# Strassen sums S3 and S4 kept in PSUM, a second copy of the high parts there, and a reordered entrance to the gate GEMM, in one decoder layer

## The chip, the cores and the metric

One core of a Trainium2 chip runs the whole program. The metric is the device time of one execution in microseconds (us); the kernel before has a median of 2184.21 us over 3 runs (2181.18 to 2185.54).

## The reference

One step of a hybrid layer with width D = 2048, for 512 prompt tokens and 8 x 4 sample tokens, 544 in all. Only the second half matters here:

```python
mixed = concat(rms_norm(a, g_attn), rms_norm(s, g_ssm)) @ w_out      # 2048 x 2048
x = x + mixed
hf = rms_norm(x, g_ffn)
x = x + (silu(hf @ w_gate) * (hf @ w_up)) @ w_down                   # D_FF = 5632
y = rms_norm(x, g_final)
```

## The kernel before

**Tokens and halves.** All 544 tokens stand in the columns of a tile of 128 x 544 (a `slot`), as two halves of 272 (`L_` and `R_`), so that one half fills part of one PSUM bank. A matrix product is made of fp32r matmuls of a 128 x 128 weight block with 272 columns.

**Two parts of each number.** Every operand is split in two: a high part (`Copy` into an fp32r tile on ScalarE) and a low part (the number less its high part, a `tensor_tensor` on VectorE). A product is high x high + high x low + low x high, three matmuls.

**Strassen units.** The products with `w_gate`, `w_up` and `w_down` use Strassen's scheme with seven products (`P1` to `P7`) over 2 x 2 blocks. The left sides of four of them are sums of weight blocks: S1 (`P5`) and S2 (`P6`) are made on GpSimd (`PT`), S4 (`P7`) and S3 (`P3`) on VectorE (`TT`), all in `sadd`; `P1`, `P2` and `P4` take raw blocks. A unit is one product over a half of the inner dimension: in the gate and up GEMMs 12 matmuls, 8 with the high part of its weights and then 4 with the low part. A `Gem` of gate or up has the 14 units of `TWO`, one of down the 7 of `ONE`. Two `Gem`s, gate and up, make a pair, and there are 22 pairs, 616 units.

**Order.** Nothing is scheduled at run time: each engine runs its instructions in the order in which the program writes them, and semaphores hold an instruction until its inputs and its buffer are ready. `stage` writes unit after unit: first what `at` holds for the unit (work on the results of earlier `Gem`s, and the splits of their sums), then the sums of a unit some places ahead (`sadd`, by `AHEAD`), the unit's matmuls (`mms`), the results that it completes (`events`: copies on ScalarE, `tensor_tensor` on VectorE), the conversion of the unit two places ahead (`conv(u + 2)`: high part, then low part), and a hook.

**Buffers.** High and low parts have three buffers each (`whi`, `wlo`), so `conv(u + 2)` needs the matmuls of unit u - 1 to be done. Sums lie in the four buffers of the tag `raw` (`sa`), but that of `P6` for the second half, which has a `slot`. Raw weights (`rw`, three buffers of 1 MB in two transfers of 512 KB) are fetched by SyncE; `conv` of a `P4` unit issues the next fetch, into the buffer whose last reader is a low part of `P4`. From the `w_out` product on, PSUM's eight banks are shared out as six for products (`mm`) and two for the rest (`ps`). A `Gem` holds three banks, X, Y and V; a pass over two column blocks of `w_out` (`gemm_pair`) takes four, and its results leave them by `tensor_tensor` on VectorE (`evac_wa`, `evac_ws`).

**The entrance.** `w_out` is done in eight passes over the attention half and eight over the state-space half, 96 matmuls each. After each of the latter, two row blocks of x get their sums and their Strassen forms (`make_forms`), and their squares go to `accA`. During the last pass unit 0 of the gate is converted, units 1 and 2 after it. `rstd_bcast` at unit 10 sums `accA` over partitions on TensorE and makes 1/sqrt of the mean (`rbf`, the tile `rbc`): two `tensor_scalar`, `Sqrt` on ScalarE, one reciprocal of 128 x 544 and four more VectorE instructions for a Newton step.

## Time and profile before

| what | us |
|---|---|
| median of 3 runs (lowest, highest) | 2184.21 (2181.18, 2185.54) |
| the profiled execution, its own time | 2186.86 |
| its span from first to last instruction | 2185.0 |
| first matmul of the gate, first of down | 686.0, 1669.6 |
| the `w_out` passes | 480 to 686 |
| TensorE, VectorE, GpSimd, ScalarE busy in the span | 2062.3, 1865.6, 1156.2, 1087.9 |

The span is the profile's; the execution's own time has 1.86 us more around it. "Busy" of TensorE is that of pipelined matmuls, so that a busy TensorE can still be one that started late. A row of a group has the source line, the engine, the operation, the tile written and the tiles read by their names in the program (`wh` high part, `wl` low part, `rw` raw weights, `sa` a sum, `s` a slot, `mm` and `ps` PSUM banks).

### The profile page before, as it was taken

How to read it: one execution, taken by the hardware profiler on the slowest of the kernel's cores; microseconds unless marked ns; L12 is line 12 of the kernel's file. 1: busy time of each engine (PE TensorE's matmuls, PEld its weight loads, DVE VectorE, ACT ScalarE, POOL GpSimd, SP SyncE). 2: the span in 40 equal slices, each digit the busy share in tenths (PEclk: the TensorE clock that was granted, in tenths of full speed). 3: DMA queues.
4: the chain of work that ended last, by engine and by line, in shares of the span. 5: the costliest groups of instructions: out<-in, count | busy, mean ns of one | idle time of the engine just before them, and what ended most of it. 6: DMA issues, size and time to landing. Idle time of an engine off the chain costs nothing.

```text
span 2185.0 us, 43831 instructions
## 1 busy us (share of the span) xinstructions
PE 2062.3 (94%) x16370; PEld 2003.8 (92%) x16370; DVE 1865.6 (85%) x2825; ACT 1087.9 (50%) x2277; POOL 1156.2 (53%) x1012
## 2 busy tenths in 40 slices
PE   8497999999998999999999999999999999999996
PEld 7497899879988899999999999999999999999996
DVE  7988845668577899999999999999988888888987
ACT  6132336765254455455555555455554545544564
POOL 7715442123275566666666666666655555555600
PEclk9798999999998999999999999999999999999998
DMA  6354793214343244434443454435349988977554
GB/s 178 98 149 148 220 294 113 76 55 130 110 135 117 78 159 142 143 123 140 161 145 120 129 173 133 133 129 173 126 145 322 329 288 280 346 267 240 191 162 144
DMA packets 331646, 368.46 MB, mean 169 GB/s; under 512 B 55473, under 2 KB 260249, under 8 KB 331417
## 3 DMA queue, kind: packets, MB, share of 16 engines
q1 hardware_dynamic: 330536, 363.92, 51.3%
q8 instruction: 129, 2.11, 0.4%
q0 software_dynamic: 640, 1.48, 0.2%
q14 instruction: 85, 0.69, 0.1%
q10 hardware_dynamic: 256, 0.26, 0.0%
HBM read 277.67 MB, written 88.52 MB: 168 GB/s over the span
## 4 chain that ended last, share of the span: by engine, by line
PE 69%; DVE 12%; issue 4%; ACT 2%; POOL 1%; DMA 1%; DVEq 0%; SPq 0%; ACTq 0%; POOLq 0%
PE mm L2009 52%; PE mm L293 14%; DVE wl L1995 4%; DVE s L388 1%; DVE sa L1976 1%; DVE sa L1978 1%; DVE wl L263 1%; POOL s L2283 1%; PE ps L1368 0%; PE ps L1626 0%; PE ps L1620 0%; ACT wh L261 0%; DMA rw<-in_w_gate_dram 0%; POOL accA L342 0%; DMA s<-fd 0%
## 5 line engine op out<-in xcount | busy, mean ns | idle before, releaser
L2009 PE MATMUL mm<-s,wh 128*128 128x272 f32 x7056 | 1040.2, 289 | 9.8 <-ACT wh L1994 4.5
L2009 PEld LDWEIGHTS mm<-s,wh 128*128 128x128 f32 x7056 | 946.5, 189 | 17.0 <-ACT wh L1994 8.8
L2009 PE MATMUL mm<-s,wl 128*128 128x272 f32 x3528 | 597.6, 291 | 20.3 <-DVE wl L1995 19.8
L293 PE MATMUL mm<-s,wh 128*128 128x272 f32 x2816 | 503.3, 298 | 36.8 <-DVE u L1158 13.5
L2009 PEld LDWEIGHTS mm<-s,wl 128*128 128x128 f32 x3528 | 499.6, 189 | 35.0 <-DVE wl L1995 34.9
L1995 DVE TENSOR_TENSOR wl<-sa,wh 128x512 fp32r<-128x512 f32 (+1 forms) x468 | 473.3, 1016 | 42.2 <-ACT wh L1994 36.8
L1995 DVE TENSOR_TENSOR wl<-rw,wh 128x512 fp32r<-128x512 f32 (+1 forms) x384 | 409.8, 1076 | 66.3 <-ACT wh L1994 62.5
L293 PEld LDWEIGHTS mm<-s,wh 128*128 128x128 f32 x2816 | 415.0, 194 | 48.2 <-issue 18.3
L1994 ACT ACTIVATE wh<-sa 128x512 fp32r<-128x512 f32 (+1 forms) x468 | 291.0, 623 | 262.6 <-PE mm L2009 108.3
L293 PE MATMUL mm<-s,wl 128*128 128x272 f32 x1408 | 314.6, 294 | 16.9 <-DVE wl L263 16.8
L1994 ACT ACTIVATE wh<-rw 128x512 fp32r<-128x512 f32 (+1 forms) x384 | 238.5, 621 | 143.2 <-PE mm L2009 96.7
L1972 POOL TENSOR_TENSOR sa<-rw 128x512 f32<-128x512 f32 (+1 forms) x128 | 204.6, 1599 | 163.9 <-DMA rw<-in_w_gate_dram 52.0
L293 PEld LDWEIGHTS mm<-s,wl 128*128 128x128 f32 x1408 | 232.8, 193 | 19.9 <-DVE wl L263 19.8
L261 ACT ACTIVATE wh<-raw 128x512 fp32r<-128x512 f32 x200 | 124.2, 625 | 164.7 <-PE mm L293 104.3
L263 DVE TENSOR_TENSOR wl<-raw,wh 128x512 fp32r<-128x512 f32 x152 | 122.8, 813 | 73.0 <-ACT wh L261 72.8
L388 DVE TENSOR_TENSOR s<-s,s 128x544 fp32r<-128x544 f32 (+2 forms) x154 | 142.7, 943 | 33.6 <-ACT s L387 27.1
L2082 POOL TENSOR_TENSOR s<-s,rbc 128x544 f32<-128x544 f32 x66 | 114.9, 1754 | 72.6 <-ACT s L2085 72.6
L1974 POOL TENSOR_TENSOR sa<-sa,rw 128x512 f32<-128x512 f32 (+1 forms) x84 | 138.9, 1653 | 3.2
L342 POOL TENSOR_TENSOR wl<-raw,wh 128x512 fp32r<-128x512 f32 x48 | 64.5, 1346 | 138.6 <-ACT wh L261 128.2
L342 POOL TENSOR_TENSOR s<-s,s 128x512 f32<-128x512 f32 (+3 forms) x67 | 79.0, 1190 | 58.2 <-ACT s L921 36.5
L2180 POOL TENSOR_TENSOR s<-s,s 128x272 f32<-128x272 f32 x40 | 30.9, 773 | 130.4 <-ACT s L2179 130.4
L1976 DVE TENSOR_TENSOR sa<-rw 128x512 f32<-128x512 f32 (+1 forms) x128 | 96.9, 757 | 0.0
(350 smaller groups left out, 2112.4 us busy)
## 6 DMA issues: line engine op xcount, KB each, us to landing
rw<-in_w_gate_dram SPq DMA_DIRECT2D x88, 512.0 KB
rw<-in_w_up_dram SPq DMA_DIRECT2D x88, 512.0 KB
rw<-in_w_down_dram SPq DMA_DIRECT2D x72, 512.0 KB
fd<-s SPq DMA_DIRECT2D x133, 272.0 KB
s<-fd SPq DMA_DIRECT2D x133, 272.0 KB
x2d<-s SPq DMA_DIRECT2D x80, 272.0 KB
s<-x2d SPq DMA_DIRECT2D x80, 272.0 KB
raw<-in_w_in_dram SPq DMA_DIRECT2D x72, 256.0 KB
```

Of the source, the lines that this page charges most:

```text
L261: nc.scalar.activation(out=hi[:, :nk], in_=t[:, :nk], func=AF.Copy)
L263: eng.tensor_tensor(out=lo[:, :nk], in0=t[:, :nk], in1=hi[:, :nk].bitcast(F32), op=ALU.subtract)
L293: nc.tensor.matmul(ps[mt][h][:, :HALF], lhsT=w, rhs=x[:, h * HALF:(h + 1) * HALF], start=st, stop=sp)
L342: return f(*a, **kw)
L388: nc.vector.tensor_tensor(out=lo, in0=src, in1=hi.bitcast(F32), op=ALU.subtract)
L1972: PT(out=v, in0=blk(g, h, 1, 0), in1=blk(g, h, 1, 1), op=ALU.add)
L1974: PT(out=v, in0=g.S[h], in1=blk(g, h, 0, 0), op=ALU.subtract)
L1976: TT(out=v, in0=blk(g, h, 0, 0), in1=blk(g, h, 1, 0), op=ALU.subtract)
L1994: nc.scalar.activation(out=hv, in_=src, func=AF.Copy)
L1995: TT(out=lv, in0=src, in1=hv.bitcast(F32), op=ALU.subtract)
L2009: nc.tensor.matmul(ps[:, :HALF], lhsT=w[:, j, :], rhs=x, start=new and i == 0, stop=last and i == len(todo) - 1, skip_group_check=True)
L2082: return lambda: PT(out=gt[t], in0=gt[t], in1=rbf, op=ALU.mult)
```

## The change

The sums for `P7` and `P3` go to a bank of `ps` in place of a `raw` buffer. In gate and up, ScalarE writes the high part of a raw block (`P1`, `P2`, `P4`) a second time, to a `ps` bank, and VectorE's subtraction reads it there. The pools become five `mm` and three `ps` banks. At the entrance, units 0 and 1 are converted during the last `w_out` pass; the last row blocks get a form routine of their own (`last`), which puts half of the forms and the squares behind the first units; `rstd_bcast` is written out in six hooks at units 8 to 13, with the reciprocal in two halves and its two partition sums in `mm` banks; and one multiplication by `rbf` in the first gate is planned three units later.

```diff
--- before.py
+++ after.py
@@ -1964,7 +1964,9 @@
     def sadd(u):
         g, p, h, _, _ = units[u]
         n = g.halves[h][1]
-        if (p, h) == ("P6", 1):
+        if p in ("P7", "P3"):
+            v = bank()[:, :n * P].rearrange("p (a c) -> p a c", c=P)
+        elif (p, h) == ("P6", 1):
             v = slot()[:, :n * P].rearrange("p (a c) -> p a c", c=P)
         else:
             v = v128(stream.tile([P, NK, 256], F32, tag="raw", name=nm("sa"), bufs=4), n)
@@ -1992,7 +1994,12 @@
         lo = stream.tile([P, NK, 256], F32R, tag="wlo", name=nm("wl"))
         hv, lv = v128(hi, n), v128(lo, n)
         nc.scalar.activation(out=hv, in_=src, func=AF.Copy)
-        TT(out=lv, in0=src, in1=hv.bitcast(F32), op=ALU.subtract)
+        if p in ("P1", "P2", "P4") and len(g.halves) == 2:
+            hp = bank()[:, :n * P].rearrange("p (a c) -> p a c", c=P)
+            nc.scalar.activation(out=hp, in_=hv.bitcast(F32), func=AF.Copy)
+        else:
+            hp = hv.bitcast(F32)
+        TT(out=lv, in0=src, in1=hp, op=ALU.subtract)
         conv_t[u] = hv, lv
         if p == "P4":
             raw_dma()
@@ -2088,7 +2095,7 @@
             TT(out=ut[1][:, L_], in0=g.b["X"][:, :HALF], in1=gt[1][:, L_], op=ALU.mult)
 
         def post_gate(u0):
-            plan_at(u0 + 11, lambda: PT(out=gt[1][:, R_], in0=gt[1][:, R_], in1=rbf[:, R_], op=ALU.mult))
+            plan_at(u0 + (14 if f == 0 else 11), lambda: PT(out=gt[1][:, R_], in0=gt[1][:, R_], in1=rbf[:, R_], op=ALU.mult))
             plan_at(u0 + 15, silu(1), None, scale(1), None, scale(0), None, silu(0), None, scale(0))
 
         def post_up(u0):
@@ -2294,6 +2301,27 @@
                     steps[:] = make_forms(xg[0], xg[1], e, xforms[m0 // 2])
                     steps[0]()
                 steps = []
+                if m0 == 14:
+                    def last():
+                        b0, b1 = xg
+                        t, v = slot(), slot()
+                        a, bh, bl, th, tl, vh, vl = (slot(F32R) for _ in range(7))
+                        split((a[:, L_], a[:, R_]), b0[:, L_])
+                        TT(out=t[:, L_], in0=b0[:, R_], in1=b0[:, L_], op=ALU.subtract)
+                        split((th[:, L_], tl[:, L_]), t[:, L_])
+                        TT(out=t[:, R_], in0=b1[:, R_], in1=t[:, L_], op=ALU.subtract)
+                        split((th[:, R_], tl[:, R_]), t[:, R_])
+                        xforms[7].extend([a, bh, bl, th, tl, vh, vl])
+
+                        def rest0():
+                            TT(out=v[:, L_], in0=b1[:, R_], in1=b0[:, R_], op=ALU.subtract)
+                            TT(out=v[:, R_], in0=b1[:, L_], in1=t[:, R_], op=ALU.subtract)
+                            split((vh, vl), v)
+                        at.setdefault(1, []).append(rest0)
+                        at.setdefault(2, []).append(lambda: split((bh, bl), b1))
+                        at.setdefault(3, []).append(squares)
+                    deferred.append(last)
+                    return
                 deferred.append(forms)
                 deferred.append(lambda: steps[1]())
                 deferred.append(lambda: steps[2]())
@@ -2302,8 +2330,8 @@
 
     es_ps.close()
     es_ps2 = ExitStack()
-    pools["mm"] = es_ps2.enter_context(tc.tile_pool(name="mm2", bufs=6, space=PSUM))
-    pools["ps"] = es_ps2.enter_context(tc.tile_pool(name="ps2", bufs=2, space=PSUM))
+    pools["mm"] = es_ps2.enter_context(tc.tile_pool(name="mm2", bufs=5, space=PSUM))
+    pools["ps"] = es_ps2.enter_context(tc.tile_pool(name="ps2", bufs=3, space=PSUM))
     AXP = Pairs(ah, al)
     for m in range(0, 16, 2):
         for mt in range(2):
@@ -2336,12 +2364,11 @@
             if k == 2:
                 for u in sum_at.pop(-1):
                     sadd(u)
-            if k == 6:
-                conv(0)
+            if k in (4, 6):
+                conv(k // 2 - 2)
 
         run(gemm_pair(SXP, evac_ws(m), pre_piece=first_units if m == 14 else None))
-    for u in range(1, 3):
-        conv(u)
+    conv(2)
     flush()
     probe("x2", x2[0])
 
@@ -2352,7 +2379,36 @@
     nc.sync.dma_start(out=v_s[0, :, 0:124].rearrange("b r h d -> b (r h d)"),
                     in_=cache_v[0, :, 4:128].rearrange("b r h d -> b (r h d)"))
 
-    units[0][0].hooks[10] = lambda: rstd_bcast(rbf, accA, D)
+    rs = {}
+
+    def rs_sum():
+        rs["p"] = [bank("mm"), bank("mm")]
+        for x in range(2):
+            nc.tensor.matmul(rs["p"][x][:, :HALF], lhsT=ones, rhs=accA[:, x * HALF:(x + 1) * HALF], start=True, stop=True)
+
+    def rs_mean():
+        rs["m"], rs["t"] = slot(), slot()
+        for x in range(2):
+            TSC(out=rs["m"][:, x * HALF:(x + 1) * HALF], in0=rs["p"][x][:, :HALF], scalar1=1.0 / D, scalar2=EPS,
+                op0=ALU.mult, op1=ALU.add)
+        nc.scalar.activation(out=rs["t"], in_=rs["m"], func=AF.Sqrt)
+
+    def rs_rec(x):
+        return lambda: nc.vector.reciprocal(out=rbf[:, x * HALF:(x + 1) * HALF], in_=rs["t"][:, x * HALF:(x + 1) * HALF])
+
+    def rs_newton(i):
+        def go():
+            m, t = rs["m"], rs["t"]
+            if i == 0:
+                TT(out=t, in0=rbf, in1=rbf, op=ALU.mult)
+                TT(out=t, in0=t, in1=m, op=ALU.mult)
+            else:
+                TSC(out=t, in0=t, scalar1=-0.5, scalar2=1.5, op0=ALU.mult, op1=ALU.add)
+                TT(out=rbf, in0=rbf, in1=t, op=ALU.mult)
+        return go
+
+    for i, f_ in enumerate((rs_sum, rs_mean, rs_rec(0), rs_rec(1), rs_newton(0), rs_newton(1))):
+        units[0][0].hooks[8 + i] = f_
     stage(0, nU - 3)
     WS.limit = len(pieces)
     w_dma(nextp[0] + 1)
```

In rows of the program's order the numbers behind a name tell one tile from another. The first place is VectorE in a gate `Gem`, from the low part of `P6`'s first half to that of `P2`'s second half. Before:

```order
L1995 TENSOR_TENSOR wl_9313<-sa_9205,wh_9312 128x512
L1978 TENSOR_TENSOR sa_9317<-rw_8935,sa_9205 128x512
L1995 TENSOR_TENSOR wl_9334<-s_9277,wh_9333 128x512
L1976 TENSOR_TENSOR sa_9340<-rw_8935 128x512
L1995 TENSOR_TENSOR wl_9356<-sa_9317,wh_9355 128x512
L1976 TENSOR_TENSOR sa_9360<-rw_9159 128x512
L1995 TENSOR_TENSOR wl_9375<-sa_9340,wh_9374 128x512
L388 TENSOR_TENSOR s_9379<-s_9177,s_9379 128x272
L1995 TENSOR_TENSOR wl_9397<-sa_9360,wh_9396 128x512
L1995 TENSOR_TENSOR wl_9414<-rw_9159,wh_9413 128x512
```

With the change:

```order
L2002 TENSOR_TENSOR wl_9346<-sa_9232,wh_9345 128x512
L1980 TENSOR_TENSOR ps_9350<-rw_8944,sa_9232 128x512
L2002 TENSOR_TENSOR wl_9367<-s_9310,wh_9366 128x512
L1978 TENSOR_TENSOR ps_9373<-rw_8944 128x512
L2002 TENSOR_TENSOR wl_9389<-ps_9350,wh_9388 128x512
L1978 TENSOR_TENSOR ps_9393<-rw_9184 128x512
L2002 TENSOR_TENSOR wl_9408<-ps_9373,wh_9407 128x512
L388 TENSOR_TENSOR s_9412<-s_9202,s_9412 128x272
L2002 TENSOR_TENSOR wl_9430<-ps_9393,wh_9429 128x512
L2002 TENSOR_TENSOR wl_9447<-rw_9184,ps_9449 128x512
```

Order and count are the same. The sums of `P3` and `P7` are now written to `ps`, the low parts of `P3` and `P7` read that bank, and the low part of `P2` reads the second copy of the high part in place of the high part; those of `P6` read two SBUF tiles as before.

The second place is ScalarE at the end of an up `Gem` and the start of the next gate: the high parts of `P3`, `P4`, `P1`, `P5`, `P2` and `P1`. Before:

```order
L1994 ACTIVATE wh_9180<-sa_9141 128x512
L1994 ACTIVATE wh_9198<-rw_8878 128x512
L1994 ACTIVATE wh_9219<-rw_8935 128x512
L1994 ACTIVATE wh_9236<-sa_9162 128x512
L1994 ACTIVATE wh_9256<-rw_8935 128x512
L1994 ACTIVATE wh_9273<-rw_9159 128x512
```

With the change, from the same high part on:

```order
L1996 ACTIVATE wh_9205<-ps_9164 128x512
L1996 ACTIVATE wh_9223<-rw_8894 128x512
L1999 ACTIVATE ps_9226<-wh_9223 128x512
L1996 ACTIVATE wh_9246<-rw_8944 128x512
L1999 ACTIVATE ps_9249<-wh_9246 128x512
L1996 ACTIVATE wh_9265<-sa_9187 128x512
L1996 ACTIVATE wh_9285<-rw_8944 128x512
L1999 ACTIVATE ps_9288<-wh_9285 128x512
```

Behind the high part of each raw block stands its second copy (L1999); what came behind it stands one place later.

The third place is VectorE at the first 1/sqrt, around units 11 to 15 of the first gate. Before:

```order
L1995 TENSOR_TENSOR wl_8875<-rw_8198,wh_8874 128x512
L1995 TENSOR_TENSOR wl_8900<-sa_8860,wh_8899 128x512
L1770 TENSOR_SCALAR s_8905<-ps_8903 128x272
L1770 TENSOR_SCALAR s_8905<-ps_8904 128x272
L400 RECIPROCAL rbc<-s_8906 128x544
L401 TENSOR_TENSOR s_8906<-rbc 128x544
L402 TENSOR_TENSOR s_8906<-s_8906,s_8905 128x544
L403 TENSOR_SCALAR s_8906<-s_8906 128x544
L404 TENSOR_TENSOR rbc<-rbc,s_8906 128x544
L2062 TENSOR_TENSOR s_8896<-mm_8736,s_8783 128x272
L1995 TENSOR_TENSOR wl_8932<-rw_8337,wh_8931 128x512
```

With the change:

```order
L2002 TENSOR_TENSOR wl_8889<-rw_8198,ps_8891 128x512
L2392 TENSOR_SCALAR s_8897<-mm_8870 128x272
L2392 TENSOR_SCALAR s_8897<-mm_8871 128x272
L2002 TENSOR_TENSOR wl_8921<-ps_8874,wh_8920 128x512
L2397 RECIPROCAL rbc<-s_8898 128x272
L2069 TENSOR_TENSOR s_8917<-mm_8736,s_8791 128x272
L2002 TENSOR_TENSOR wl_8939<-rw_8337,ps_8941 128x512
L2397 RECIPROCAL rbc<-s_8898 128x272
L2002 TENSOR_TENSOR wl_8963<-rw_8503,ps_8965 128x512
L2403 TENSOR_TENSOR s_8898<-rbc 128x544
L2404 TENSOR_TENSOR s_8898<-s_8898,s_8897 128x544
L2072 TENSOR_TENSOR s_8917<-mm_8713,s_8846 128x272
```

The reciprocal is two instructions of 272 columns, and between the parts of the computation stand results (L2069, L2072) and low parts of the units that follow.

## Rows read from the trace of the kernel before

**Rows 1.** Gate and up: busy us and count of PE, PEld, DVE, ACT, POOL.

```profile
730.60:1669.60 939.00, 925.93 (x7202) 907.54 (x7201) 877.57 (x981) 488.37 (x896) 603.61 (x419) 1.00 0.44 145
```

**Rows 2.** Strassen matmuls and weight loads by stretch; granted clock behind the counts.

```profile
686.00:730.60 44.60, 32.02 (x192) 30.70 (x193) 0.81 0.24 83
730.60:1669.60 939.00, 925.93 (x7202) 907.54 (x7201) 1.00 0.44 145
1700.00:2000.00 300.00, 300.00 (x2399) 300.00 (x2398) 1.00 0.87 299
...
1021.48:1029.08 7.60, 7.05 (x50) 6.21 (x49) 1.00 0.00 1
```

**Rows 3.** Waits, 860 to 1640 us: total us, times, longest.

```profile
PEld mm L2009 <- DVE wl L1995: 23.0, 56, 1.4
...
PE mm L2009 <- DVE wl L1995: 10.5, 29, 1.2
PEld mm L2009 <- ACT s L2054: 3.4, 16, 0.5
```

**Rows 4.** Timeline, up to a gate's units 4 to 8: start, duration, instruction.

```profile
1006.36 1.78 DVE L1995 TENSOR_TENSOR wl<-rw,wh 128x512 fp32r<-128x512 f32 x1
...
1010.00 0.94 SPq L1951 DMA_DIRECT2D rw<-in_w_gate_dram  x2
...
1015.45 1.29 POOL L1972 TENSOR_TENSOR sa<-rw 128x512 f32<-128x512 f32 x1 [3.18 <-DVE wl L1995]
...
1023.88 1.09 POOL L2117 TENSOR_TENSOR s<-s,s 128x272 f32<-128x272 f32 x1
...
1024.40 0.77 PE L2009 MATMUL mm<-s,wl 128*128 128x272 f32 x4 [0.26 <-DVE wl L1995]
...
1026.64 1.77 DVE L1995 TENSOR_TENSOR wl<-sa,wh 128x512 fp32r<-128x512 f32 x1
```

**Rows 5.** By line, 860 to 1640 us: count, shortest, median, longest in ns.

```profile
L2062 DVE TENSOR_TENSOR s<-mm,s x35: 426/428/430, 877.4 to 1623.9; 128x272 f32<-128x272 f32 x35
...
L1995 DVE TENSOR_TENSOR wl<-sa,wh x251: 676/1032/1853, 859.4 to 1639.2; 128x512 fp32r<-128x512 f32 x126
L1995 DVE TENSOR_TENSOR wl<-rw,wh x212: 676/948/1789, 860.4 to 1629.4; 128x512 fp32r<-128x512 f32 x106
...
L1994 ACT ACTIVATE wh<-rw x212: 613/632/637, 861.1 to 1639.3; 128x512 fp32r<-128x512 f32 x106
```

**Rows 6.** Timeline of the entrance and of the first 1/sqrt.

```profile
692.88 2.18 PE L2009 MATMUL mm<-s,wh 128*128 128x272 f32 x8 [3.44 <-ACT wh L1994]
...
698.49 1.39 PE L2009 MATMUL mm<-s,wh 128*128 128x272 f32 x8
...
717.01 3.55 DVE L400 RECIPROCAL rbc<-s 128x544 f32<-128x544 f32 x1 [0.72 <-ACT s L399]
...
718.65 1.16 PE L2009 MATMUL mm<-s,wh 128*128 128x272 f32 x8
...
724.82 1.27 PE L2009 MATMUL mm<-s,wl 128*128 128x272 f32 x4 [5.01 <-DVE wl L1995]
```

**Rows 7.** Timeline of results leaving the banks at two ends of `w_out` passes.

```profile
506.30 0.67 PE L293 MATMUL mm<-s,wh 128*128 128x272 f32 x4
...
508.58 0.78 DVE L1859 TENSOR_TENSOR s<-mm,s 128x272 f32<-128x272 f32 x2
...
509.07 0.99 PE L293 MATMUL mm<-s,wh 128*128 128x272 f32 x4 [1.11 <-DVE s L1859]
...
629.27 0.67 PE L293 MATMUL mm<-s,wh 128*128 128x272 f32 x4
...
630.86 1.47 DVE L2280 TENSOR_TENSOR s<-mm,rbc 128x272 f32<-128x272 f32 x4
```

**Rows 8.** Timeline of a last-chunk down `Gem`.

```profile
2014.01 2.17 DVE L1995 TENSOR_TENSOR wl<-sa,wh 128x384 fp32r<-128x384 f32 x2
...
2017.97 0.99 PE L2009 MATMUL mm<-s,wh 128*128 128x272 f32 x6 [0.41 <-DVE s L2192]
```

## The prediction

> **What bounds the kernel now.** I read first how long the Strassen matmuls take in each stretch, then who was waited for, then the timeline where the waits lie.
>
> In down, from 1700 to 2000 us, TensorE is busy for all of 300 us over 2399 matmuls, 125 ns each [rows 2]; 12 of them, a unit that waits for nothing, take 1.50 us (I use 1.504, with which units in a row follow each other). The 600 units of gate and up from 730.6 us on would take 902.4 us and take 939.0 [rows 2]: 36.6 us are lost, 1.71 a pair. The first 16 units, from 686.0 to 730.6, take 44.6 us in place of 24.1: 20.5 lost, at a granted clock of 0.81, so a part of them ran at the lower of its two levels, 1.2 and 2.4 GHz [rows 2].
>
> The waits name one thing: between 860 and 1640 us TensorE and its weight loads waited for a low part made on VectorE (10.5 and 23.0 us; the two overlap), and 3.4 us for a result leaving bank X [rows 3]. VectorE is busy for 877.6 of 939.0 us [rows 1], 20.5 us in a `Gem` whose matmuls need 21.1.
>
> The loss sits in one place. The four gate units from 1021.48 to 1029.08 (`P6`, `P6`, `P3`, `P7`) take 7.60 us, 1.58 over their four times 1.504 [rows 2], nearly a pair's whole loss. There VectorE's instructions and GpSimd's sums alternate, and VectorE's instructions of 512 columns last up to 1.8 us [rows 4].
>
> **Reading from PSUM.** Low parts of 512 columns last 676 ns at the shortest, with a median of 948 to 1032 and up to 1853; results with one operand in PSUM (272 columns) last 426 to 430 ns in all 35 cases, although GpSimd is busy 64% of this time [rows 1, 5]. So an instruction with two SBUF operands is held up by GpSimd, one with a PSUM operand is not. A 512-column low part that reads PSUM isn't in the trace: it costs 0.68 us if it is never held, 1.03 if nothing changes; I take 0.68, since the PSUM rows have no spread at all. Per `Gem`, six low parts of raw blocks go from 0.95 to 0.68 and those of `P7` and `P3`, four, from 1.03: 3.0 us of VectorE's 20.5.
>
> The Trainium skill (SBUF — State Buffer, Who interferes with whom) has it that a VectorE instruction with two SBUF inputs and a GpSimd instruction that reads SBUF exclude each other for a whole instruction, while one with at most one SBUF input stays out of it. By that rule, which the trace bears out, the low parts of `P5` and `P6` and the sums themselves stay as long as they are; that is the second case below.
>
> **Gate and up: -30.** Only what ends last counts. (a) `P7`'s low part at 1026.64 took 1.77 us, against a sum of GpSimd, and TensorE got it 0.55 late [rows 4]. At 0.68 it is in time: 0.55 of the 1.58, safe. (b) The other 1.0 hangs on `P6`'s second low part, still two SBUF operands, which TensorE got 0.4 late at 1024.40, and on what queues behind it: `P3`'s low part, and ScalarE's copy of X, which stands behind a high part that waits for a sum. It was slow because GpSimd's chain of sums ran until 1024.97 (L2117). That chain starts when the gate's second raw block has landed, 1015.45 (L1972; the profile names a low part that ended at that moment, but other sums of this line wait for the fetch by name), and its fetch was issued at 1010.00, behind `P4`'s low part of the up `Gem` [rows 4]. In front of that low part stand a low part of 1.78 us [rows 4] and others of the same kind, now 0.68 each, less 0.6 for the second copy: the fetch goes out some 1.5 us sooner, the chain ends near 1023, and the low part then needs no alternating. It would be ready at about 1023.6, needed at 1024.0. That leaves little room, so I leave 0.3 of a pair's 1.7: 1.4 x 21.4 pairs = 30 us. Bounds: (a) alone, 0.55 x 21.4 = 12; everything, 36.6.
>
> **What the second copies cost: 0.** Six copies of 0.63 us [rows 5] a `Gem` take ScalarE from 488 of 939 us [rows 1] to some 650, 72% of the shorter stage. A raw unit's chain is high part 0.63, copy 0.63, low part 0.68; it starts when a `whi` buffer comes free, two units before its own, and its low part is wanted 8 matmuls into that unit: 2 x 1.50 + 1.0 = 4.0 us for 1.9 of work. That slack of 2 us is the cover. How long an ACTIVATE into PSUM or a VectorE sum into PSUM lasts the trace doesn't show: 0.40 times 512/272 = 0.75 would be the nearest guess from the 272-column copies, and even a copy twice as long stays inside the slack. A bank of `ps` comes round after three allocations, ten a `Gem`, so each is free two units after its use; if VectorE is that late, ScalarE stands, and the copies of X, Y behind it too.
>
> **Entrance: -5.5.** Unit 1 began at 692.88, after 3.44 us without work, because its high part stood behind the last pass's results [rows 6]. Now units 0 and 1 run before that gap and unit 2 starts there, 1.5 us won. But the forms behind it now go to and fro between VectorE and ScalarE piece by piece (sum, high part, low part), so unit 3 starts late: unit 2's high part, copy and low part end at 694.1, four sums and two splits of 272 columns follow at 0.43 each with 0.4 of ScalarE between, and the high part is ready at about 698.8, where unit 3 started at 698.49 [rows 6]. That takes the gain back. The squares' two ScalarE instructions and half of the forms stand behind units 3 and 4, worth 1 to 2: I take 1.5 (0 to 6). At the 1/sqrt the reciprocal of 3.55 us and what follows it kept a low part back for 5.01 us [rows 6], after which the clock was low; units 13 to 15 took from 718.65 [rows 6] to 730.6, 7.4 more than their 4.5. The same work, 8 us, is now spread over five units, of which each leaves VectorE about 0.9 us beside a lead of 2; by that some 3.5 us of stalls remain, each near 1 us, as long as those in gate and up [rows 3], where the clock stays at 1.00 [rows 2]. So -4 (-2 to -7). The two partition sums take `mm` banks, but bank X of the next `Gem` gets a bank that is free by then.
>
> **`w_out` with five banks: +3.3.** A pass needs four banks at once. With six, a pass's first two were always free; with five, its second matmul waits for the first result of the pass before. That result left at 509.01 (508.58 plus 0.43) where the pass began at 506.30: a wait of 2.6, in place of one 13 matmuls on that ended at 509.07 [rows 7]. At 630.86 plus 0.43 it is 1.9 for a pass begun at 629.27, where 1.0 was lost anyway. Going so through the 15 boundaries, seven wait more than before: 1.0, 0.3, 0.25, 0.7, 0.9, 0 (a wait that comes later takes it in) and 0.2, together 3.3. Bounds: 0, if the waits behind take them in, and 16 times the longest.
>
> The Trainium skill (Perfetto Trace Analysis, Optimizing Tensor Performance, on matmuls) wants groups that don't depend on each other to rotate through different banks, so that one's results leave during the next one's matmuls, and five banks for passes of four go against it. By the rule each boundary is exposed, the third case; the rows above show seven of them that are.
>
> **Down: -3.** In the last chunk's eight `Gem`s, TensorE waits 0.41 us for a result queued on VectorE behind low parts (2.17 us for two, at 2014.01) [rows 8]. These two are `P7` and `P3`, now PSUM: 8 x 0.4 = 3.2. Bounds 0 and 3.3.
>
> **Sum.** -30 - 5.5 + 3.3 - 3 = -35. From the profiled execution (2185.0 span, 1.86 around it, 2186.9) that is 2151.7; the median of the runs is 2.65 lower: **2149**.
>
> **The rivals.**
> 1. As summed, 2149: 0.60.
> 2. VectorE stays the bound in the gate's four units, because low parts of `P5` and `P6`, form splits and sums still alternate with GpSimd: (a) alone, -12.4, entrance -5.5, `w_out` +3.3, down 0: -14.6, 2170. For it: the five VectorE instructions that end with the first late low part all keep two SBUF operands. Against: GpSimd's chain starts sooner. 0.22.
> 3. Slower: the banks. If each of the 16 `w_out` passes waits as long as the worst (2.6 us), 42 us are lost in place of 3.3: 2188. It ends on that side from an average of 2.4 us a pass. Against: most results left within 0.5 us of their last matmul. 0.05.
> 4. The change doesn't do what it says, since PSUM operands of 512 columns or copies into PSUM are slow, and low parts come as late as before: entrance and `w_out` only, -2: 2182. 0.07.
> 5. All of it: -36.6 - 12 + 3.3 - 3 = -48, 2136. 0.06.
>
> Cases 1, 2 and 5 are faster by over 0.2% (4.4 us, about what can be told from no change here): 0.88; within, 0.07; slower, 0.05. The range goes from the last case with a few us of spread, 2132, to the second, 2173; case 1 alone has 2138 to 2160.
>
> **What would show it.** Right: low parts from `rw` and `ps` at 0.68 without spread, those of `P5`, `P6` still spread; the waits for low parts in gate and up down from 23 to under 6 us; the stage from the first matmul of the gate to the first of down down from 983.6 to about 948; unit 2 starting where unit 1 did; no wait of 5 us at the reciprocal; new short waits for VectorE's results at `w_out` boundaries. Wrong: copies into PSUM well over 0.7 us, ScalarE waiting for `ps` banks, or GpSimd's chain still ending after the low part of `P6`.

## The result

The changed kernel takes 2145.97 us (median of 4 runs, 2141.46 to 2146.99) against 2183.94 of the kernel before beside it: a ratio of 0.9823, 95% interval 0.9806 to 0.9841. The prediction was 2149 in a range of 2132 to 2173.

The profiled execution has a span of 2143.9 us. These are windows of its Strassen matmuls, cut at the first matmul of gate unit 0, unit 16, unit 28 (the second pair) and of down, then one window of the `w_out` matmuls. Behind the length of each stand busy time and count of PE and PEld, the granted clock, the DMA share and GB/s:

```profile
684.64:722.22 37.58, 29.09 (x192) 27.27 (x193) 0.91 0.21 71
722.22:742.81 20.59, 18.84 (x147) 18.19 (x146) 1.00 0.21 62
742.81:1632.66 889.85, 888.73 (x7058) 886.32 (x7057) 1.00 0.45 151
1632.66:2038.12 405.46, 402.97 (x3194) 402.09 (x3192) 1.00 0.83 283
```

```profile
474.45:684.64 210.19, 200.75 (x1536) 198.46 (x1536) 0.97 0.41 129
```

The 21 pairs from unit 28 on are 588 units, 884.4 us without a loss. Before, they took 939.0 [rows 2] less 18.0 for units 16 to 27, that is 921.0, or 1.74 lost a pair; now it is 889.9, or 0.26. Set beside the terms of the prediction:

| stretch | before | after | difference | predicted |
|---|---|---|---|---|
| `w_out` | 207.05 | 210.19 | +3.1 | +3.3 |
| gate units 0 to 27 (the entrance) | 62.65 | 58.17 | -4.5 | -5.5 |
| 21 pairs | 921.0 | 889.85 | -31.1 | -30 |
| down | 408.8 | 405.46 | -3.3 | -3 |

These come to -35.8, where -35 was forecast. The profiled spans differ by 5 us more, 4.5 of it ahead of `w_out`, which the change doesn't touch: that stretch took 479.0 us in the profile of before, 474.5 here, 472 to 479 in the experiments.

The waits over 780 us of gate and up, as long as [rows 3] (total us, times, longest):

```profile
POOL sa L1974 <- DVE wl L2002: 7.7, 3, 3.2
...
PEld mm L2016 <- DVE wl L2002: 1.4, 2, 0.7
PE mm L2016 <- DVE wl L2002: 1.0, 2, 0.5
PEld mm L2016 <- ACT s L2061: 0.9, 5, 0.2
```

The waits for low parts, 23.0 and 10.5 before, are gone but for two. The same stretch by line (count, shortest, median, longest in ns) answers to [rows 5], and one window (PE, PEld, DVE, ACT, POOL) to [rows 1]:

```profile
L2002 DVE TENSOR_TENSOR wl<-rw,ps x220: 669/686/690, 824.6 to 1593.0; 128x512 fp32r<-128x512 f32 x110
L2002 DVE TENSOR_TENSOR wl<-ps,wh x148: 672/678/694, 823.2 to 1602.2; 128x512 fp32r<-128x512 f32 x148
L2002 DVE TENSOR_TENSOR wl<-sa,wh x111: 677/843/1858, 827.2 to 1596.4; 128x512 fp32r<-128x512 f32 x111
...
L1999 ACT ACTIVATE ps<-wh x220: 601/602/605, 824.0 to 1592.4; 128x512 f32<-128x512 f32 x110
...
L1978 DVE TENSOR_TENSOR ps<-rw x74: 681/685/1784, 837.1 to 1600.2; 128x512 f32<-128x512 f32 x74
```

```profile
823.00:1603.00 780.00, 779.02 (x6190) 777.24 (x6190) 621.66 (x846) 543.62 (x992) 456.44 (x363) 1.00 0.44 146
```

A low part with an operand in PSUM has no spread; one with two in SBUF (`sa`) still has. A sum that only writes to PSUM (L1978) has it too, up to 1784 ns: what counts is where the inputs lie. VectorE went from 93% busy to 80, ScalarE to 70 (72 was forecast).

The place of [rows 4] in the changed kernel, where unit 5 (`P6`) starts at 1004.67 (1021.48 before):

```profile
991.36 0.94 SPq L1951 DMA_DIRECT2D rw<-in_w_gate_dram  x2
...
996.85 1.30 POOL L1974 TENSOR_TENSOR sa<-rw 128x512 f32<-128x512 f32 x1 [2.17 <-DMA rw<-in_w_gate_dram]
...
1004.51 1.11 POOL L2124 TENSOR_TENSOR s<-s,s 128x272 f32<-128x272 f32 x1
1004.55 1.07 PEld L2016 LDWEIGHTS mm<-s,wh 128*128 128x128 f32 x8
1004.67 1.17 PE L2016 MATMUL mm<-s,wh 128*128 128x272 f32 x8
1004.87 0.40 ACT L2057 ACTIVATE s<-mm 128x272 f32<-128x272 f32 x1 [0.59 <-PE mm L2016]
1004.91 1.27 DVE L2002 TENSOR_TENSOR wl<-s,wh 128x512 fp32r<-128x512 f32 x1
...
1005.59 1.73 POOL L1974 TENSOR_TENSOR sa<-rw 128x512 f32<-128x512 f32 x1
...
1006.10 1.77 DVE L1978 TENSOR_TENSOR ps<-rw 128x512 f32<-128x512 f32 x1
```

Against the start of unit 5, the fetch goes out 13.3 us ahead (11.5 before), GpSimd's first sum on the block starts 7.8 ahead (6.0), its chain (L2124) ends 0.95 behind (3.5), and the second low part of `P6` ends 1.5 behind, where it is wanted at 2.5 and came at 2.9. So the sooner fetch is there, and named now by the profile as what GpSimd waited for. But that low part still took 1.27 us: it was in time because it started sooner, not because it was free of GpSimd. And the collision that had been that of `P7`'s low part is now that of `P7`'s sum (1006.10, against GpSimd's next sum at 1005.59).

### The profile page after: what moved, and what is told of

It is laid out like the page before. It is cut to its first block, busy times and chain, and to the rows that moved or that the text cites. A ratio compares the mean times of both kernels' runs of the same rounds, so it can differ in the third digit from the quotient of the medians.

```text
span 2143.9 us, 44033 instructions
## 1 busy us (share of the span) xinstructions
PE 2043.3 (95%) x16370; PEld 2002.5 (93%) x16370; DVE 1659.7 (77%) x2827; ACT 1233.6 (58%) x2542; POOL 1060.1 (49%) x1012
## 3 DMA queue, kind: packets, MB, share of 16 engines
q0 software_dynamic: 640, 1.48, 0.2%
## 4 chain that ended last, share of the span: by engine, by line
PE 79%; DVE 6%; ACT 2%; issue 2%; POOL 1%; DMA 0%; SPq 0%; ACTq 0%; DVEq 0%; POOLq 0%
PE mm L2016 60%; PE mm L293 15%; DVE s L388 1%; DVE wl L263 1%; DVE wl L2002 1%; PE ps L1368 1%; PE ps L1626 0%; PE ps L1620 0%; POOL s L2290 0%; ACT wh L261 0%; DMA s<-fd 0%; PE ps L1387 0%; ACT s L1750 0%; PE ps L2440 0%; PE ps L1408 0%
## 5 line engine op out<-in xcount | busy, mean ns | idle before, releaser
L2002 DVE TENSOR_TENSOR wl<-rw,ps 128x512 fp32r<-128x512 f32 x264 | 180.8, 685 | 121.8 <-ACT ps L1999 118.4
L1974 POOL TENSOR_TENSOR sa<-rw 128x512 f32<-128x512 f32 (+1 forms) x128 | 175.9, 1374 | 118.3 <-DMA rw<-in_w_up_dram 68.1
L2002 DVE TENSOR_TENSOR wl<-ps,wh 128x512 fp32r<-128x512 f32 (+1 forms) x256 | 173.3, 677 | 68.6 <-ACT wh L1996 66.3
L1996 ACT ACTIVATE wh<-sa 128x512 fp32r<-128x512 f32 (+1 forms) x212 | 132.0, 624 | 107.4 <-PE mm L2016 97.9
L2002 DVE TENSOR_TENSOR wl<-sa,wh 128x512 fp32r<-128x512 f32 (+1 forms) x212 | 183.0, 866 | 13.2 <-ACT wh L1996 12.5
L1996 ACT ACTIVATE wh<-ps 128x512 fp32r<-128x512 f32 (+1 forms) x256 | 150.8, 589 | 68.1 <-PE mm L2016 29.6
L1999 ACT ACTIVATE ps<-wh 128x512 f32<-128x512 f32 x264 | 159.0, 602 | 8.4
L388 DVE TENSOR_TENSOR s<-s,s 128x544 fp32r<-128x544 f32 (+2 forms) x155 | 127.2, 836 | 35.5 <-ACT s L387 29.0
L2002 DVE TENSOR_TENSOR wl<-rw,wh 128x512 fp32r<-128x512 f32 (+1 forms) x120 | 125.8, 1048 | 29.9 <-ACT wh L1996 29.9
L2089 POOL TENSOR_TENSOR s<-s,rbc 128x544 f32<-128x544 f32 x66 | 107.6, 1644 | 71.8 <-ACT s L2092 71.8
```

The lines of the kernel that those rows point to most:

```text
L388: nc.vector.tensor_tensor(out=lo, in0=src, in1=hi.bitcast(F32), op=ALU.subtract)
L1974: PT(out=v, in0=blk(g, h, 1, 0), in1=blk(g, h, 1, 1), op=ALU.add)
L1996: nc.scalar.activation(out=hv, in_=src, func=AF.Copy)
L1999: nc.scalar.activation(out=hp, in_=hv.bitcast(F32), func=AF.Copy)
L2002: TT(out=lv, in0=src, in1=hp, op=ALU.subtract)
L2089: return lambda: PT(out=gt[t], in0=gt[t], in1=rbf, op=ALU.mult)
```

## The experiments

All runs in one table: the median, the ratio to the kernel before beside it, and from each profile the `w_out` stage, units 0 to 27, the 21 pairs, what a pair loses ((21 pairs - 884.4) / 21), and down, in us.

| run | time | ratio, 95% | `w_out` | units 0-27 | 21 pairs | a pair | down |
|---|---|---|---|---|---|---|---|
| changed kernel | 2145.97 | 0.9806-0.9841 | 210.2 | 58.2 | 889.9 | 0.26 | 405.5 |
| copy_sbuf | 2172.48 | 0.9935-0.9968 | 209.9 | 60.3 | 915.6 | 1.49 | 405.4 |
| sums_only | 2157.41 | 0.9871-0.9902 | 207.7 | 58.4 | 903.1 | 0.89 | 404.8 |
| copies_only | 2148.16 | 0.9829-0.9859 | 209.9 | 58.8 | 885.8 | 0.07 | 410.0 |
| fetch_late | 2163.76 | 0.9902-0.9931 | 209.9 | 58.3 | 908.7 | 1.16 | 406.8 |
| best62 | 2138.53 | 0.9784-0.9814 | 207.0 | 58.8 | 886.2 | 0.09 | 405.3 |
| entr_before | 2179.59 | 0.9973-0.9996 | 207.1 | 59.6 | 919.0 | 1.65 | 409.9 |
| rstd_old | 2145.73 | 0.9817-0.9846 | 207.7 | 61.6 | 891.6 | 0.35 | 403.9 |
| all_copies | 2137.58 | 0.9775-0.9815 | 207.7 | 57.9 | 884.8 | 0.02 | 404.0 |
| sa_held | 2145.89 | 0.9797-0.9840 | 210.0 | 58.0 | 888.7 | 0.21 | 404.7 |
| best | 2135.68 | 0.9765-0.9796 | 211.6 | 53.4 | 884.8 | 0.02 | 404.6 |
| best3 | 2137.25 | 0.9778-0.9805 | 207.1 | 57.7 | 884.8 | 0.02 | 404.9 |
| late_all | 2141.14 | 0.9795-0.9822 | 207.7 | 58.0 | 885.0 | 0.03 | 406.2 |

A stage repeats from profile to profile much more closely than the whole time does (`w_out` with five banks apart, which takes either 207.7 or some 210), so that differences under 4 us are read from the stages.

**Is it the operand in PSUM, or only a second instruction on ScalarE?** (copy_sbuf)

```diff
-            hp = bank()[:, :n * P].rearrange("p (a c) -> p a c", c=P)
+            hp = slot()[:, :n * P].rearrange("p (a c) -> p a c", c=P)
```

> The second copy of the high part goes to an SBUF tile in place of a PSUM bank; ScalarE does the same instructions in the same order, the sums of P3 and P7 stay in PSUM. Theory (an operand in PSUM keeps the low part from being held up by GpSimd): the low parts of raw blocks are spread again, with a median near 0.95 us, the fetch goes out about 1 us later than in the changed kernel, and the stretch from the first gate matmul to the first of down is 958 to 970 us in place of 948.0; the time 2156 to 2168. Rival (it is the second instruction on ScalarE, which starts the low part later, wherever it writes): the stretch stays at 948 to 951, the time at 2146 to 2149.

Of the 31 us gained on the 21 pairs, 26 are lost again; the time is above the 2156 to 2168 of the theory, and farther still from the rival. By line, 860 to 1600 us (count, busy us, mean ns, then the idle time before):

```profile
L2002 DVE TENSOR_TENSOR wl<-rw,s 128x512 fp32r<-128x512 f32 x204 | 192.6, 952 | 71.2 <-ACT s L1999 67.5 <-PE mm L2016 2.7
```

The same subtraction with both operands in SBUF has a mean of 952 ns, though its median is 694 (near 950 was expected). It also waits for the copy, so it ends later than without one: a copy that doesn't change where the operand lies costs (1.49 a pair, against 0.89 with no copy at all, below).

**The sums alone, the copies alone.** (sums_only, copies_only)

```diff
-        if p in ("P1", "P2", "P4") and len(g.halves) == 2:
+        if False:
```

> The changed kernel without the second copies: the low parts of raw blocks read the high part in SBUF as before; the sums of P3 and P7 stay in PSUM, and so do banks and entrance. Theory (the sums are worth term (a), the copies the sooner fetch, term (b)): steady gate and up gains 12 of the 28.6 us, the stretch from the first gate matmul to the first of down is about 965, the time about 2163. Rival 1 (the sums carry the whole gain): 948 and 2146. Rival 2 (they carry nothing): 977 and 2175.

```diff
-        if p in ("P7", "P3"):
-            v = bank()[:, :n * P].rearrange("p (a c) -> p a c", c=P)
-        elif (p, h) == ("P6", 1):
+        if (p, h) == ("P6", 1):
```

> The changed kernel with the sums of P3 and P7 back in their SBUF buffers, in down too; the second copies of the high parts, banks and entrance stay. Theory (copies alone give the sooner fetch, term (b), of 1.0 to 1.4 us a pair; the low part of P7 stays 0.55 late): the stretch from the first gate matmul to the first of down is about 955 to 960, down is 3 us longer, the time 2156 to 2161. Rival (the late low parts are the same ones, and the copies alone clear them): 948 to 950, the time 2149 to 2151.

The sums alone bring 17.9 us of the 31.1 on the 21 pairs, where term (a) allowed 12. The copies alone bring 35.2, more than both together: here the rival is right. The steady windows of sums_only and copies_only:

```profile
738.72:1641.78 903.06, 895.60 (x7058) 887.29 (x7057) 1.00 0.45 150
```

```profile
741.60:1627.38 885.78, 885.49 (x7059) 884.95 (x7057) 1.00 0.45 152
```

So (a) and (b) aren't two losses with a cure each. With the copies alone, `P7`'s low part has two SBUF operands again and lasts 1.78 us (medians of the 21 pairs), but it ends 0.62 us before it is wanted: it starts sooner, with all that stands before it. Here it is in one pair of copies_only, beside a sum of GpSimd, and the matmuls that read it:

```profile
1131.26 1.68 POOL L1972 TENSOR_TENSOR sa<-rw 128x512 f32<-128x512 f32 x1 [1.83 <-DVE wl L2000]
...
1131.70 1.78 DVE L2000 TENSOR_TENSOR wl<-sa,wh 128x512 fp32r<-128x512 f32 x1
...
1134.10 0.66 PE L2014 MATMUL mm<-s,wl 128*128 128x272 f32 x4
```

Before, the same low part took as long (1.77 us, at 1026.64 [rows 4]) and was late. The sums in PSUM are worth something in down (405.5 against 410.0) and nothing in gate and up beside the copies.

**Does the loss hang on the fetch?** (fetch_late)

```diff
+        if pend:
+            gg, hh = pend.pop()
+            nc.vector.tensor_copy(junk, blk(gg, hh, 1, 1)[:, 0, 0:1])
+            raw_dma()
         if p == "P4":
-            raw_dma()
+            if len(g.halves) == 2:
+                pend.append((g, h))
+            else:
+                raw_dma()
```

> The changed kernel with each fetch of raw weights in gate and up issued one unit (1.5 us) later: VectorE reads one column of the block once more, behind the low part of the unit that follows P4, and the buffer is released by that; nothing else changes. Theory (term (b): the gate's loss hangs on when GpSimd's chain of sums starts, and that on the fetch): GpSimd's chain ends about 1.5 us later against the gate's units, the second low part of P6 is held up again, and a part of the 1.0 us a pair comes back: the stretch from the first gate matmul to the first of down is 955 to 970, the time 2153 to 2168. Rival (shorter instructions on VectorE alone carry the gain): within 2 us of 948.0, the time 2146 to 2148.

```profile
741.51:1650.17 908.66, 902.56 (x7058) 889.51 (x7057) 1.00 0.44 148
```

The theory holds: low parts that read PSUM are as short as in the changed kernel (a mean of 686 ns), the fetch goes out a unit later, and 18.8 us are back, 0.9 a pair. GpSimd's chain ended 2.1 us later against the gate's units (median of 19 pairs).

**A low part with two SBUF operands, or a sum that comes late?** (all_copies, late_all)

```diff
-        if p in ("P1", "P2", "P4") and len(g.halves) == 2:
+        if p not in ("P7", "P3") and len(g.halves) == 2:
```

> The changed kernel with a second copy in PSUM for P5 and P6 of gate and up as well, so that every low part there has one operand in PSUM. Theory (the low parts with two SBUF operands are what is still held up): they last 0.68 us, the 0.26 us a pair that is still lost goes under 0.1, the stretch from the first gate matmul to the first of down 944 to 946 in place of 948.0. Rival (14 tiles a Gem go through three ps banks, and ScalarE has ten copies of 0.6 us more to do a Gem: it is late, and the high parts with it): 955 or more, the time 2153 or more.

> The kernel with all copies, with each fetch in gate and up one unit (1.5 us) later, by the same edit that cost the changed kernel 0.9 us a pair. Theory (a late fetch costs because GpSimd's chain of sums then holds up low parts with two SBUF operands; with one operand in PSUM in each, it no longer does): a pair loses 0.2 us or less, the stretch from the first gate matmul to the first of down is 943 to 948, the time 2138 to 2143. Rival (the sums themselves come too late for the high parts, or VectorE's sums of P3 and P7 are what is held up): 0.8 to 1.2 a pair as with the changed kernel, 960 or more, the time 2153 or more.

With an operand in PSUM in every low part, nothing is lost in 588 units, and the ten copies a `Gem` (six in the changed kernel) cost nothing. By line and by window:

```profile
L2002 DVE TENSOR_TENSOR wl<-sa,ps x112: 676/689/690, 822.7 to 1602.2; 128x512 fp32r<-128x512 f32 x112
```

```profile
738.82:1623.62 884.80, 884.80 (x7059) 884.80 (x7057) 1.00 0.45 152
```

And late_all, with the same late fetch that cost the changed kernel 18.8 us, loses 0.2:

```profile
738.56:1623.52 884.96, 884.96 (x7058) 884.85 (x7057) 1.00 0.45 152
```

This settles the mechanism. The late fetch moves GpSimd's chain as far there (its end against unit 5 goes from 0.2 us behind in all_copies to 2.3, as it goes from 0.8 in the changed kernel to 3.0 in fetch_late; medians of 19 pairs), and TensorE doesn't notice; the one-column copies that the edit adds cost nothing either. A late fetch costs only where GpSimd's chain then meets low parts with two SBUF operands.

**Why do the sums in PSUM cost something beside the copies?** (sa_held; each sum of `P7` and `P3` also takes a `raw` buffer, `d`, and `conv` reads it behind the low part)

```diff
+        if p in ("P7", "P3") and len(g.halves) == 2:
+            d = stream.tile([P, NK, 256], F32, tag="raw", name=nm("sa"), bufs=4)
+            nc.vector.tensor_copy(d[:, 0, 0:1], v[:, 0, 0:1])
+            held[u] = d
```

> The changed kernel, sums of P3 and P7 in PSUM, but each also takes one of the four SBUF sum buffers of gate and up as before: VectorE writes one column into it behind the sum and reads it behind the low part, so that GpSimd finds no free buffer sooner than without the change. Theory (with those buffers free, GpSimd's first sum for the next block starts at once when its chain ends, 2.3 us into unit 4 in place of 4.2, meets the sum of P7 on VectorE, and that is why PSUM sums beside the copies lose 0.26 us a pair against 0.07 without them): GpSimd's sum is back near 4.2, a pair loses 0.05 to 0.12, the stretch from the first gate matmul to the first of down 944 to 946 in place of 948.0. Rival (writing sums to PSUM, or three banks for ten tiles, costs it): 0.26 a pair and 948 as before.

Half of it holds. GpSimd's first sum for the next block is held back, to 4.7 us into unit 4, and 16 of the 21 pairs lose 0.02, where eleven of the changed kernel's lose 0.05 to 0.2. But five pairs lose 0.6 to 1.1, so that the mean is 0.21, outside the theory's 0.05 to 0.12. A part of what sets such pairs apart is seen best in copies_only: two of 21 pairs lose anything (0.75 and 0.27), and they are the two in which GpSimd's first sum on the gate's second block starts latest, 5.1 and 5.7 us ahead of unit 4 against 6.2 to 6.6. In sa_held it explains three of the five (4.7 to 4.8 ahead); the other two have that sum 6.1 ahead, as pairs do that lose nothing. Here is that sum with its fetch in a pair that loses nothing and in the next one, which loses 0.75:

```profile
1157.42 0.94 SPq L1951 DMA_DIRECT2D rw<-in_w_gate_dram  x2
...
1162.78 1.31 POOL L1972 TENSOR_TENSOR sa<-rw 128x512 f32<-128x512 f32 x1 [1.71 <-DMA rw<-in_w_gate_dram]
...
1199.55 0.94 SPq L1951 DMA_DIRECT2D rw<-in_w_gate_dram  x2
...
1206.29 1.30 POOL L1972 TENSOR_TENSOR sa<-rw 128x512 f32<-128x512 f32 x1 [3.09 <-DMA rw<-in_w_gate_dram]
```

The fetches are issued 42.13 us apart, a pair's length; from issue to sum the one takes 5.4 us, the other 6.7. How many such pairs an execution has was seen in one profile of each kernel, so how much of 0.26 against 0.07 is the sums' doing stays open.

**The entrance.** (entr_before: before with the diff's parts at 2088, 2294, 2336 and 2352 alone; rstd_old: the changed kernel with this)

```diff
-            plan_at(u0 + (14 if f == 0 else 11), lambda: PT(out=gt[1][:, R_], in0=gt[1][:, R_], in1=rbf[:, R_], op=ALU.mult))
+            plan_at(u0 + 11, lambda: PT(out=gt[1][:, R_], in0=gt[1][:, R_], in1=rbf[:, R_], op=ALU.mult))
...
-    for i, f_ in enumerate((rs_sum, rs_mean, rs_rec(0), rs_rec(1), rs_newton(0), rs_newton(1))):
-        units[0][0].hooks[8 + i] = f_
+    units[0][0].hooks[10] = lambda: rstd_bcast(rbf, accA, D)
```

> The kernel before with the entrance edits alone (units 0 and 1 converted in the last pass, the form routine of the last row blocks, 1/sqrt in six hooks, the multiplication by rbf three units later); low parts, sums and banks as before. Theory (the entrance gains by its order alone): the first 16 gate units take 38 to 40 us in place of 44.6, the rest of gate and up 939 as before, the time 2176 to 2179. Rival (a good part of the 7.0 us gained there came from the quicker low parts and sums): 41 to 44, the time 2180 to 2184.

> The changed kernel with the 1/sqrt in one piece at unit 10 again and the multiplication by rbf at its old place; all else as changed. Theory (most of the entrance's gain is the 1/sqrt spread over units): the first 16 units take 41 to 44 us in place of 37.6, with one wait of 3 to 5 us behind the reciprocal, and the time is 2149 to 2153. Rival (the order of the forms gives the gain, and quicker low parts take in the 1/sqrt): 37 to 39, the time 2146 to 2147.

The first 16 units of entr_before and of rstd_old:

```profile
681.75:720.15 38.40, 28.82 (x192) 27.42 (x193) 0.87 0.21 70
```

```profile
680.11:723.63 43.52, 31.20 (x193) 29.57 (x194) 0.80 0.18 62
```

Both theories hold for the first 16 units: the order alone gives 6.2 of the 7.0, and 5.9 return with the 1/sqrt in one piece. The times don't follow: entr_before lies 0.6 above the theory's 2179, and rstd_old is within 0.3 of its rival's 2146. But a cut at unit 16 flatters the change. Over 28 units the entrance edits alone give 3.1 of the 4.5 (59.6 against 62.65), and the 1/sqrt is worth 3.4 (61.6 against 58.2), since the changed kernel loses 2.6 at units 16 and 17, where rstd_old loses nothing. The timeline of the changed kernel shows both sides:

```profile
714.19 1.84 DVE L2397 RECIPROCAL rbc<-s 128x272 f32<-128x272 f32 x1
...
716.84 1.84 DVE L2397 RECIPROCAL rbc<-s 128x272 f32<-128x272 f32 x1
...
721.62 0.77 PE L2016 MATMUL mm<-s,wl 128*128 128x272 f32 x4 [0.57 <-DVE wl L2002]
...
723.30 1.28 ACT L2092 ACT_TABLE_LOAD   x1 [4.42 <-DVE s L2086]
...
725.82 1.27 PE L2016 MATMUL mm<-s,wh 128*128 128x272 f32 x8 [1.18 <-ACT wh L1996]
```

No wait of 5 us is left; but ScalarE stands for 4.42 us in front of the silu of the gate's result, which needs `rbf`, finished later now, and the high part behind it comes 1.18 late. The medians of rstd_old and the changed kernel (2145.7 and 2146.0) don't show it, since stages that the edit leaves alone moved the other way (`w_out` 2.5 and down 1.6 shorter).

**A version from the parts that paid.** best62 has the copies, the sums in PSUM in down alone, and six and two banks throughout:

```diff
-        if p in ("P7", "P3"):
+        if p in ("P7", "P3") and len(g.halves) == 1:
...
-    pools["mm"] = es_ps2.enter_context(tc.tile_pool(name="mm2", bufs=5, space=PSUM))
-    pools["ps"] = es_ps2.enter_context(tc.tile_pool(name="ps2", bufs=3, space=PSUM))
+    pools["mm"] = es_ps2.enter_context(tc.tile_pool(name="mm2", bufs=6, space=PSUM))
+    pools["ps"] = es_ps2.enter_context(tc.tile_pool(name="ps2", bufs=2, space=PSUM))
```

> Second copies in gate and up as in the changed kernel, but the sums of P3 and P7 go to PSUM in down alone, and the pools stay at six mm and two ps banks throughout; the entrance is that of the changed kernel. From the runs so far, by parts: w_out back to what it takes with six banks (207.1 in place of 210.2), the stretch from the first gate matmul to the first of down as without PSUM sums there (944.6 in place of 948.0), down as in the changed kernel (405.4 against 410.0 without PSUM sums). Theory (these parts add up, and two ps banks are enough for six copies a Gem): about 2139 to 2142, faster than the changed kernel by 4 to 7. Rival (two ps banks are too few: ScalarE waits for one at each copy and copies of results are late): gate and up over 950, the time 2146 or more.

```profile
473.29:680.30 207.01, 199.39 (x1536) 197.23 (x1536) 0.98 0.41 131
```

Right in each part, and its slowest run (2140.43) is below the fastest of the changed kernel (2141.46). The next two also have the copies for `P5` and `P6`, and convert unit 2 between the last pass's results. best keeps the sums in PSUM and reopens the pools, six and two in `w_out`, as five and three after `flush()` (the last line below is in best alone), and plans the first gate's silu chain two units later; best3 keeps best62's banks and sums.

```diff
+            if m == 14:
+                conv(2)
...
-    conv(2)
     flush()
+    es_ps2.close()
```

> Second copies in PSUM for P5 and P6 too; six mm and two ps banks during w_out, five and three from the gate on; unit 2 converted between the results of the two row blocks of the last pass; the first gate's silu chain planned two units later. From the kernel with all copies (2137.6), by parts: w_out 3.1 less, unit 2 at once behind unit 1 and unit 3 1.1 sooner, the 2.1 us lost before unit 17 down to 0.5. Theory (the parts add up): 2130 to 2134; w_out 207.1 or 204.8, the first 16 units 36 to 37 us, the rest of gate and up about 904. Rival (the new pools wait for the last results of w_out, and the entrance loses there what w_out gains): the first 16 units 39 or more, the time 2137 or more.

> Six mm and two ps banks throughout; sums of P3 and P7 in SBUF in gate and up, in PSUM in down; second copies for P5 and P6 as well, so that gate and up take ten tiles a Gem from two banks, all of them copies; unit 2 converted between the results of the two row blocks of the last pass; the rest as changed. Theory (w_out as with six banks, 207.0; the gate's first matmul no longer waits for reopened pools; unit 2 follows unit 1, and unit 3 starts 1.1 sooner; no loss in steady gate and up): the first 16 units 36 to 37.5 us, the rest of gate and up 905 to 906, the time 2133 to 2137. Rival (two banks are too few for a copy at each unit but P3 and P7): a pair loses 0.3 or more and the rest of gate and up is 911 or more, the time 2141 or more.

In best the reopened pools made the gate's first matmul wait for the last results, as its rival has it (the wait is in its 211.6 for `w_out`), and units 0 to 27 are 4.5 us shorter than in all_copies for what was prepared meanwhile; the silu chain took its 2.1 us along, from unit 16 to 18:

```profile
683.92 2.15 PE L2016 MATMUL mm<-s,wh 128*128 128x272 f32 x8 [4.67 <-ACT s L2294]
```

The time of best lies between theory and rival. In best3 unit 3 starts 1.5 sooner than in the changed kernel and units 16 to 18 give 1.4 of it back; its time is 0.3 above the theory's. Two banks are enough. The intervals of best62, all_copies, best and best3 overlap, so these don't rank them; against the changed kernel's, those of best and best3 lie below it, the other two overlap its lower end. Against the kernel before, best62 is the smallest edit of the four.

## Why the prediction was right, step by step

**What bounds the kernel** was read rightly: low parts that come late, at the gate's units 5 to 8. all_copies makes every low part quick and loses nothing.

**Reading from PSUM, 0.68 us without spread**: 686 and 678 ns in 368 low parts, where the guess came from 272-column results [rows 5]. The rule of the Trainium skill (SBUF — State Buffer, Who interferes with whom) holds in each form tried: two SBUF inputs are held up even when the result goes to PSUM (L1978, up to 1784 ns), one isn't.

**Gate and up, -30**: -31.1 on the 21 pairs. The size is right and (b) is shown: the fetch goes out 1.8 us sooner (1.5 was forecast), and fetch_late, which delays it by a unit, gives back 0.9 of a pair's 1.48. Two steps failed all the same. "The low part then needs no alternating" is wrong: it lasted 1.27 us and was ready by starting 1.4 sooner. And (a), "at 0.68 it is in time", named as safe, was not the cause: copies_only has `P7`'s low part at 1.78 us and in time. That the two together came to 30 was luck in part: each alone brings more than its share (17.9 and 35.2). I had taken each late low part as a loss of its own; they stood in one queue, and what moved the front of it moved them all.

**Second copies, 0**: 602 ns each (0.75 was the guess), and over the 780 us of gate and up no wait of TensorE for ScalarE's high parts. VectorE waits for the copies instead (97.0 us); it is idle for a fifth of the time, and copies_only, with the same copies, loses 0.07 a pair.

**Entrance, -5.5**: -4.5. Unit 2 starts 7.2 us behind the gate's first matmul, where unit 1 stood 6.9 behind it before [rows 6], and unit 3 gains nothing, both as forecast. The forms were put at -1.5 and are worth -1.1 (62.65 against 61.6 in rstd_old), the 1/sqrt at -4 and is worth -3.4; "some 3.5 us of stalls remain" came out, but most of it at units 16 and 17 and through ScalarE, which that step didn't name.

**`w_out`, +3.3**: +3.1, and best62 takes it away. The worst boundary, put at 2.6, where the pass had waited later and less [rows 7]:

```profile
504.23 0.78 DVE L1859 TENSOR_TENSOR s<-mm,s 128x272 f32<-128x272 f32 x2
...
504.72 0.65 PE L293 MATMUL mm<-s,wh 128*128 128x272 f32 x3 [2.49 <-DVE s L1859]
```

Pass by pass the boundaries cost what was added up: six passes are longer than before, by 1.2, 0.4, 0.4, 0.8, 0.3 and 0.2 us, 3.4 together (the fifth had been put at 0.9). So the Trainium skill's rule on banks (Perfetto Trace Analysis, Optimizing Tensor Performance) holds at the boundaries where VectorE is behind, and not, as the third case had it, at each. The seventh boundary, put at 0, opens the 14th pass. That pass before, in the changed kernel and in rstd_old (length, PE and PEld busy, clock):

```profile
642.26:661.74 19.48, 14.55 (x99) 13.76 (x98) 0.91 0.59 183
```

```profile
641.03:660.14 19.11, 15.19 (x99) 14.75 (x98) 0.82 0.65 201
```

```profile
638.70:655.60 16.90, 12.85 (x98) 12.19 (x97) 1.00 0.53 174
```

Inside it TensorE waits for a high part, 4.1 us before and 3.0 with five banks, and what follows runs at either level of the clock. In four of the nine profiles with five banks it was the upper level and the stage took 207.7 us, 0.7 more than with six. That the net of this profile, +3.1, is so near to 3.3 is luck to that extent; the boundaries' own 3.4 is not.

**Down, -3**: -3.3, and 4.5 back when the sums leave PSUM (copies_only).

**The rivals.** The second (VectorE stays the bound) was wrong about this kernel but right about its fragility: with the fetch 1.5 us later the 21 pairs are back at 908.7, of the 909 that (a) alone would leave. (Its sum takes 12.4 for (a), where 0.55 x 21.4 gives 11.8.) The fourth asked for slow copies into PSUM or slow reads from there; neither is slow, and copy_sbuf shows what is left when the copies don't change the operand's place. The predicted time was 3 us above the median. The terms make up 0.8 of that. For the rest, the profiled execution that I started from was long by some 4.5 us in a stretch that no term is about, and I had taken off only 2.65: its 479.0 us ahead of `w_out` came again in one of the twelve experiments, the others took 472 to 475.

## What to carry to other kernels

Where GpSimd holds VectorE up, put one operand of the instructions that must be in time into PSUM, and check by a copy to SBUF that it is the place which pays. Losses that stand in one queue don't add up by cause: before pricing each, ask what starts the queue, here a fetch that waits for a buffer. A stage that is shortened by spreading work has to be measured past the point where the last of that work is used.

## What was not expected of the hardware

The same wait was followed by either level of TensorE's clock. In the 14th pass of `w_out` TensorE waits 3.0 us in the changed kernel and in rstd_old; in the five us around the wait's end the granted clock is 0.54 of full speed, mostly the level of 1.2 GHz, in the first and 1.00, the level of 2.4 GHz, in the second (PE, PEld, DVE, ACT and POOL busy, then the clock):

```profile
650.00:655.00 5.00, 3.60 (x16) 3.60 (x17) 3.71 (x4) 2.38 (x5) 3.01 (x2) 0.54 0.39 126
```

```profile
648.00:653.00 5.00, 3.79 (x28) 3.58 (x29) 3.39 (x4) 2.54 (x5) 3.02 (x2) 1.00 0.37 117
```

This makes the `w_out` stage 207.7 in place of some 210 with five banks. And fetches of the same size, issued in the same order, let GpSimd start 1.4 us later in a single pair (copies_only, above), nearly as much as the whole change moved them.
